# Hybrid decoder trunk: v, gate values and dt computed with tokens on partitions, small matmuls in clusters, output projection in half inputs for six tiles

## The chip, the cores and the metric

One core of one Trainium2 chip runs the whole program in one launch. TensorE (PE) multiplies, VectorE (DVE), ScalarE (ACT) and GpSimd (POOL) work on the results, SyncE (SP) issues the weight transfers. The metric is the device time in microseconds (us) of one execution; the time before is the median of three runs.

## The reference

The trunk has two layers over 512 tokens of width 1024, all in float32: a half-step gated FFN, a mixer, another half-step FFN. The change is in the mixer:

```python
h = rmsnorm(x, mix_norm[l])
proj = h @ w_in[l]        # z 512 | xBC 1024 | dt 8 | q 256 | k 128 | v 128 | u 256 | gv 256
y_ssd = ssd_mixer(z, xBC, dt, ...)       # conv + silu; dt = softplus(dt + bias); chunks of 128 tokens
y_att = rmsnorm(swa_attention(q, k, v, sinks, rel_bias), attn_out_norm[l])
y_sgu = rmsnorm(chunk_sgu(u, gv, ...), sgu_out_norm[l])   # gv = layernorm(gelu(gv)), mixed over tokens
x = x + concat([y_ssd, y_att, y_sgu]) @ w_out[l]
```

In `ssd_mixer`, four chunks of 128 tokens carry a state from one to the next, and the result is multiplied by `silu(z)` and normalised. `swa_attention` works on four blocks of 128 queries.

## The kernel before

**Layout.** The residual lies as eight tiles `xT[j]` of 128 channels by 512 tokens. Each operand of a product is split into a rounded part and a rest (`whi` and `wlo` of the weights, `xhi` and `xlo` of the input: ACT makes the first, L149 and L158, DVE the second, L150 and L159). A product is three matmuls per 128 input channels: whi·xhi (L176), whi·xlo (L177), wlo·xhi (L179). An output tile of the projection, 128 channels by 512 tokens, is thus 24 matmuls of 512 columns.

**Input projection.** `in_products` runs three tiles interleaved over the first six input tiles, then the rest one by one. The order is dt, k, v, q0, q1, eight tiles of xBC, gv0, gv1, u0, u1, z0 to z3. dt is a tile of 16 outputs (rounded part and rest beside each other), 16 matmuls. The RMS factor of the tokens, `R`, comes from squares (ACT), their sum (POOL, L200), a matmul with ones (L217), a power on POOL (L221) and four matmuls that spread it over partitions (L230).

**Turning.** Products come with channels on partitions. dt (L699), v (L858) and the gate values gv (L935) are wanted with tokens on partitions: PE transposes them 128 tokens at a time against the identity, and ACT or DVE read them back.

**Small matmuls.** A list `jobs` hangs work behind each tile's emission. An attention block is scores (L875), softmax on DVE and ACT, transposes (L898), values (L904). A chunk of the SSD is transposes of x (L765) and B (L779), C·B (L776), decay on DVE, POOL and ACT (L784 to L794), the carried state (L801), the new state (L812) and the diagonal part (L807). L957 mixes gate values. L875 uses 64 of the array's rows; L686, L807, L904 and L957 fill 64 of its columns.

**Order.** The Tile framework puts the instructions of each engine in order by its own estimate of when each is ready; each engine then runs its list in that order. So a small matmul stands between product matmuls wherever it was expected to be ready.

**Output projection.** Four output tiles first take input tiles 4 to 7 (attention and gating, 12 matmuls each), while the SSD's norm is finished; then the same four take input tiles 0 to 3, then four tiles take all eight. The SSD's sum of squares (`sst`) is added on POOL.

Of the kernel before, what the change touches and what calls it, by code (L numbers as in the profile page):

```python
# [19 lines left out]
F32 = mybir.dt.float32  # L20
# [6 lines left out]
P = 128  # L27
# [21 lines left out]
XBC_AT, GV_AT, U_AT, Z_AT = 4, 12, 14, 16  # L49
# [3 lines left out]
def trunk(ctx: ExitStack, tc: tile.TileContext, a: dict, out: bass.AP, phases=None):  # L53
# [133 lines left out]

    class Stat:
# [63 lines left out]
    def in_products(tiles, xs, emit, hooks, levels=None, feed=None, ready=2, lead=3, then=None):  # L252
# [29 lines left out]
        for n in range(len(tiles) - lead):  # L282
            wt, m = nxt
            b = accbank()
            product(b[0:m, :], wt, xs, [(k, k) for ks in levels for k in ks], k0, k1)
            if lead + n + 1 < len(tiles):
                nxt = tiles[lead + n + 1]()
            elif then:
                nxt = then()
            emit(lead + n, b)  # L290
# [361 lines left out]
    def mixer(l):  # L652
# [3 lines left out]
        with tc.tile_pool(name="mp", bufs=1) as mp:  # L656
# [37 lines left out]
            def emit_dt(b):  # L694
                dtc = mp.tile([16, T], F32, name="dtc", tag="tmp", bufs=2)
                nc.vector.tensor_tensor(out=dtc, in0=b[0:16, :], in1=R[0:16, :], op=ALU.mult)
                tb = bank()[:, 0:64].rearrange("p (c e h) -> p c e h", c=NB, e=2)
                for c in range(NB):
                    nc.tensor.transpose(tb[:, c, :, :], dtc[:, c * P:(c + 1) * P], ident[0:16, 0:16])  # L699
                v, s, s2, po = (small(n, 32) for n in ("sp_v", "sp_s", "sp_q", "sp_p"))  # L700
                nc.scalar.activation(out=nega, in_=nega, func=AF.Exp)
                nc.vector.tensor_tensor(out=c8(v), in0=tb[:, :, 1, :],
                                        in1=dtb.unsqueeze(1).broadcast_to([P, NB, 8]), op=ALU.add)
                nc.vector.tensor_tensor(out=c8(v), in0=tb[:, :, 0, :], in1=c8(v), op=ALU.add)
# [8 lines left out]
                for n in (15, 13, 11, 9, 7, 5, 3):  # L713
# [6 lines left out]
                                               op0=ALU.mult, op1=ALU.mult)  # L720
                ab = bank()
# [36 lines left out]
            def ssd_chunk(c):  # L758
                if c == 0:
                    nc.scalar.activation(out=eb, in_=eb, func=AF.Exp)  # L760
                cs = slice(c * P, (c + 1) * P)
                h8 = slice(c * 8, c * 8 + 8)
                xb = bank()
                for j in range(4):
                    nc.tensor.transpose(xb[:, j * P:(j + 1) * P], xj[j][:, cs], ident)  # L765
                v64 = lambda t: t.rearrange("p (h d) -> p h d", h=8)
                xdt = t512("xdt", 2)
                nc.vector.tensor_tensor(out=v64(xdt), in0=v64(xb),
                                        in1=dt[:, h8].unsqueeze(2).broadcast_to([P, 8, 64]), op=ALU.mult)
                if c < NB - 1:  # L770
                    xde = t512("xde")
                    nc.vector.tensor_tensor(out=v64(xde), in0=v64(xb),
                                            in1=dtde[:, h8].unsqueeze(2).broadcast_to([P, 8, 64]), op=ALU.mult)
                gb = bank()
                for g in range(2):
                    nc.tensor.matmul(gb[:, g * P:(g + 1) * P], BT[g][:, cs], CT[g][:, cs], start=True, stop=True)  # L776
                if c < NB - 1:
                    for g in range(2):
                        nc.tensor.transpose(gb[:, 256 + g * P:256 + (g + 1) * P], BT[g][:, cs], ident)  # L779
                n = 512 if c < NB - 1 else 256  # L780
                cbt = t512("cbt", 2)
                nc.scalar.copy(out=cbt[:, 0:n], in_=gb[:, 0:n])
                acb = mp.tile([P, 8, P], F32, name="acb", tag="acb", bufs=2)
                nc.gpsimd.dma_start(out=acb, in_=arow[l][h8, :].partition_broadcast(P))  # L784
                dec = []
                for g in range(2):
# [6 lines left out]
                    nc.scalar.activation(out=dg, in_=dg, func=AF.Exp)  # L793
                    nc.vector.tensor_tensor(out=dg, in0=dg,  # L794
                                            in1=cbt[:, g * P:(g + 1) * P].unsqueeze(1).broadcast_to([P, 4, P]),
                                            op=ALU.mult)
                    dec.append(dg)
# [7 lines left out]
                yb = bank()  # L805
                for h in range(8):
                    nc.tensor.matmul(yb[(h % 2) * 64:(h % 2 + 1) * 64, (h // 2) * P:(h // 2 + 1) * P],  # L807
                                     xdt[:, h * 64:(h + 1) * 64], dec[h // 4][:, h % 4, :], start=True, stop=True)
                if c < NB - 1:
# [11 lines left out]
                    state["prev"] = pv  # L821
                for j in range(4):
                    nc.vector.scalar_tensor_tensor(out=xj[j][:, cs], in0=xj[j][:, cs], scalar=vcol(R_DS + l * 4 + j),
                                                   in1=yb[:, j * P:(j + 1) * P], op0=ALU.mult, op1=ALU.add)
# [4 lines left out]

            def emit_z(j, b):  # L830
                z = mp.tile([P, T + 3], F32, name="z", tag=("xc", "cv")[j // 2], bufs=2)[:, 0:T]
                nc.vector.tensor_tensor(out=z, in0=b, in1=R, op=ALU.mult)
                nc.scalar.activation(out=z, in_=z, func=AF.Silu)
                nc.vector.tensor_tensor(out=xj[j], in0=xj[j], in1=z, op=ALU.mult)
                sst.add(xj[j])
# [17 lines left out]
            def emit_v(b):  # L853
                v = t512("v", 2, "tmp")
                nc.vector.tensor_tensor(out=v, in0=b, in1=R, op=ALU.mult)
                tb = bank()
                for c in range(NB):
                    nc.tensor.transpose(tb[:, c * P:(c + 1) * P], v[:, c * P:(c + 1) * P], ident)  # L858
                nc.scalar.copy(out=vt.rearrange("p c d -> p (c d)"), in_=tb)

# [3 lines left out]
            def att_block(n):  # L864
# [26 lines left out]
                nc.vector.reciprocal(out=dn, in_=dn)  # L891
                for kv in range(2):
                    pb = bank()[:, 0:2 * W].rearrange("p (g k q) -> p g k q", g=2, k=nk)
                    for g in range(2):
                        nc.vector.tensor_scalar(out=s[kv][:, g, :], in0=s[kv][:, g, :],
                                                scalar1=dn[:, 2 * kv + g:2 * kv + g + 1], scalar2=None, op0=ALU.mult)
# [3 lines left out]
                    nc.scalar.copy(out=pT, in_=pb)  # L900
                    ob = bank()
# [18 lines left out]
            gvs = []  # L920

            def emit_gv(i, b):
                g = t512("gvt", 2, "tmp")
                nc.vector.tensor_tensor(out=g, in0=b, in1=R, op=ALU.mult)
                nc.scalar.activation(out=g, in_=g, func=AF.Gelu_apprx_tanh)
                gvs.append(g)

            def sgu_norm():
                bks = [bank(), bank()]
                mv = mp.tile([P, NB, 2], F32, name="mv")  # L930
                rs = small("rs", NB)
                for c in range(NB):
                    tb = bks[c // 2][:, (c % 2) * 256:(c % 2 + 1) * 256]
                    for i in range(2):
                        nc.tensor.transpose(tb[:, i * P:(i + 1) * P], gvs[i][:, c * P:(c + 1) * P], ident)  # L935
                    bst = mp.tile([P, 6], F32, name="bst", tag="bst", bufs=2)
                    nc.vector.bn_stats(out=bst, in_=tb)
# [3 lines left out]
                for c in range(NB):  # L941
                    tb = bks[c // 2][:, (c % 2) * 256:(c % 2 + 1) * 256]
                    nc.vector.tensor_scalar(out=gn[:, c, :], in0=tb, scalar1=mv[:, c, 0:1], scalar2=rs[:, c:c + 1],
                                            op0=ALU.subtract, op1=ALU.mult)
# [7 lines left out]
            def sgu_mix(i):  # L952
                b = bank().rearrange("p (c t) -> p c t", c=NB)
# [17 lines left out]
            def mk_dt():  # L971
                raw = load(a["w_dt"][l]).rearrange("p (k n) -> p k n", n=8)
                w = wtile("whi")[:, :KD * 16].rearrange(
                    "p (k n) -> p k n", k=KD)
                nc.scalar.copy(out=w[:, :, 0:8], in_=raw)
                nc.vector.tensor_tensor(out=w[:, :, 8:16], in0=raw, in1=w[:, :, 0:8].bitcast(F32), op=ALU.subtract)
                return (w, None), 16

            jobs = [(mk_dt, emit_dt, [])]
            jobs.append((mk_cols(0), emit_k, []))  # L980
            jobs.append((mk_cols(1), emit_v, []))
            jobs.append((mk_cols(2), lambda b: emit_q(0, b), []))
            jobs.append((mk_cols(3), lambda b: emit_q(1, b), [L(att_block, 0)]))
            after = {0: [L(att_block, 1)], 2: [L(att_block, 2)], 4: [L(att_block, 3)], 5: [sgu_weights],
                     6: [att_stat], 7: [L(ssd_chunk, 0)]}
            for t in range(8):
                jobs.append((mk_cols(XBC_AT + t), lambda b, t=t: emit_xbc(t, b),
                             after.get(t, [])))
            jobs.append((mk_cols(GV_AT), lambda b: emit_gv(0, b), [L(ssd_chunk, 1), ast.start]))
            jobs.append((mk_cols(GV_AT + 1), lambda b: emit_gv(1, b), [L(ssd_chunk, 2), sgu_norm, att_finish]))  # L990
            uj = [(mk_cols(U_AT), lambda b: emit_u(0, b), [L(sgu_mix, 0), L(ssd_chunk, 3)]),
                  (mk_cols(U_AT + 1), lambda b: emit_u(1, b), [L(sgu_mix, 1)])]
            zj = []
# [5 lines left out]
            def emit(n, b):  # L999
                jobs[n][1](b)  # L1000
                for f in jobs[n][2]:
                    f()
# [140 lines left out]
```

## Time and profile before

| | |
|---|---|
| median of three runs (lowest, highest) | 1812.48 us (1812.39, 1815.73) |
| the profiled execution, its span | 1812.49 us, 1810.8 us |
| PE busy, DVE, ACT, POOL | 99%, 74%, 49%, 6% of the span |
| granted TensorE clock, mean | 0.999 |
| mixer of layer 0, of layer 1 (first mixer product to first product of the next FFN) | 358.54 to 559.44, 1248.22 to 1449.74 |

Times of instructions are from the start of the span. A matmul's record runs from its start to a modelled end that lies inside its successor's; how long the engine needs for one in a row of them is the distance between two starts. A matmul of float32 operands leaves two records, one for each of its two passes; a transpose and a product matmul leave one. Some records are missing.

### The profile page before, as it was taken

The numbers are of one execution on the slowest core, as the hardware profiler recorded it, in microseconds if no ns is written. First come the engines' busy times: TensorE is split into PE (matmuls) and PEld (weight loads), VectorE is DVE, ScalarE is ACT, GpSimd is POOL, SyncE is SP. The second block draws the span as 40 slices with busy tenths as digits, with TensorE's granted clock in tenths as the row PEclk, the third lists the DMA queues.
The fourth block names the chain that finished last, engine by engine and source line by source line (L and its number), as shares of the span: only waits on it lengthen the run. The fifth ranks groups of instructions, "written<-read, shape, count | busy, mean of one in ns | idle before, by whom it ended". The sixth has DMA issues, their size and how long they took to land.

```text
span 1810.8 us, 28970 instructions
## 1 busy us (share of the span) xinstructions
PE 1796.4 (99%) x11618; PEld 1614.9 (89%) x11618; DVE 1342.0 (74%) x2075; ACT 884.3 (49%) x1380; POOL 110.7 (6%) x113
## 2 busy tenths in 40 slices
PE   9999999999999999999999999999999999999998
PEld 7899989877888999989989999898788889999886
DVE  7978796568857988886688878855788589887422
ACT  5455563447444545463435555534564445546312
POOL 0000001020221000001000000010102200000000
PEclk9999999999999999999999999999999999999999
DMA  5333333342222233333313333333422223333331
GB/s 176 125 104 106 97 108 111 116 124 72 80 92 77 100 105 105 98 106 114 105 58 117 107 104 108 110 97 106 123 93 70 87 65 117 105 106 105 97 103 47
DMA packets 54963, 183.27 MB, mean 101 GB/s; under 512 B 7211, under 2 KB 9196, under 8 KB 54828
## 3 DMA queue, kind: packets, MB, share of 16 engines
q1 hardware_dynamic: 49484, 172.37, 29.1%
q0 software_dynamic: 1920, 6.59, 1.2%
q10 hardware_dynamic: 3424, 2.46, 0.5%
q8 instruction: 91, 1.49, 0.3%
q14 instruction: 44, 0.36, 0.1%
HBM read 178.48 MB, written 2.92 MB: 100 GB/s over the span
## 4 chain that ended last, share of the span: by engine, by line
PE 88%; DVE 6%; issue 2%; DMA 2%; ACT 1%; POOL 1%; POOLq 0%; ACTq 0%; SPq 0%
PE accb L176 9%; PE accb L177 9%; PE accb L179 9%; PE accb L450 8%; PE accb L452 8%; PE accb L451 8%; PE mxb L452 7%; PE mxb L450 7%; PE mxb L451 7%; PE mxb L1044 1%; PE mxb L176 1%; PE mxb L1043 1%; PE mxb L177 1%; PE mxb L179 1%; PE mxb L1042 1%
## 5 line engine op out<-in xcount | busy, mean ns | idle before, releaser
L450 PE MATMUL accb<-as,whi 128*128 128x256 f32 x1208 | 342.0, 283 | 0.0
L451 PE MATMUL accb<-as,whi 128*128 128x256 f32 x1208 | 341.7, 283 | 0.0
L452 PE MATMUL accb<-as,wlo 128*128 128x256 f32 x1208 | 341.3, 283 | 0.0
L149 ACT CAST whi<-raw 128x1024 fp32r<-128x1024 f32 (+2 forms) x161 | 161.7, 1011 | 293.8 <-PE accb L177 150.8
L150 DVE TENSOR_TENSOR wlo<-raw,whi 128x1024 fp32r<-128x1024 f32 (+2 forms) x161 | 189.0, 1180 | 125.4 <-ACT whi L149 124.6
L176 PE MATMUL accb<-xhi,whi 128*128 128x512 f32 (+1 forms) x712 | 280.8, 395 | 0.0
L177 PE MATMUL accb<-xlo,whi 128*128 128x512 f32 (+1 forms) x712 | 279.6, 393 | 0.0
L179 PE MATMUL accb<-xhi,wlo 128*128 128x512 f32 x696 | 273.0, 393 | 0.4 <-DVE wlo L150 0.3
L450 PEld LDWEIGHTS accb<-as,whi 128*128 128x128 f32 x1208 | 231.9, 192 | 0.9 <-issue 0.5
L451 PEld LDWEIGHTS accb<-as,whi 128*128 128x128 f32 x1208 | 231.9, 192 | 0.3
L452 PEld LDWEIGHTS accb<-as,wlo 128*128 128x128 f32 x1208 | 231.7, 192 | 0.0
L430 DVE TENSOR_TENSOR wlo<-tmp,whi 128x1024 fp32r<-128x1024 f32 x166 | 201.8, 1218 | 37.9 <-ACT whi L424 37.9
L452 PE MATMUL mxb<-as,wlo 128*128 128x256 f32 x784 | 222.1, 283 | 0.9 <-DVE wlo L430 0.9
L450 PE MATMUL mxb<-as,whi 128*128 128x256 f32 x784 | 222.5, 284 | 0.0
L451 PE MATMUL mxb<-as,whi 128*128 128x256 f32 x784 | 221.7, 283 | 0.0
L424 ACT CAST whi<-tmp 128x1024 fp32r<-128x1024 f32 x166 | 173.8, 1051 | 73.3 <-PE accb L177 17.1
L430 DVE TENSOR_TENSOR wlo<-raw,whi 128x1024 fp32r<-128x1024 f32 x83 | 101.6, 1224 | 109.7 <-ACT whi L424 109.7
L177 PEld LDWEIGHTS accb<-xlo,whi 128*128 128x128 f32 (+1 forms) x712 | 132.4, 186 | 29.0 <-issue 1.3
L176 PEld LDWEIGHTS accb<-xhi,whi 128*128 128x128 f32 (+1 forms) x712 | 132.3, 186 | 28.9 <-issue 1.0
L179 PEld LDWEIGHTS accb<-xhi,wlo 128*128 128x128 f32 x696 | 130.7, 188 | 28.9 <-DVE wlo L150 1.5
L452 PEld LDWEIGHTS mxb<-as,wlo 128*128 128x128 f32 x784 | 150.3, 192 | 1.5 <-DVE wlo L430 1.5
L450 PEld LDWEIGHTS mxb<-as,whi 128*128 128x128 f32 x784 | 150.3, 192 | 1.0
(284 smaller groups left out, 3434.0 us busy)
## 6 DMA issues: line engine op xcount, KB each, us to landing
raw<-in_ffn_w_up_dram SPq DMA_DIRECT2D x88, 512.0 KB, 3.5
raw<-in_ffn_w_gate_dram SPq DMA_DIRECT2D x87, 512.0 KB, 3.5
raw<-in_ffn_w_down_dram SPq DMA_DIRECT2D x48, 512.0 KB, 3.7
raw<-in_w_in_dram SPq DMA_DIRECT2D x40, 512.0 KB, 3.5
raw<-in_last_w_down_dram SPq DMA_DIRECT2D x22, 512.0 KB, 3.6
raw<-in_ffn_w_down_dram SPq DMA_DIRECT2D x24, 384.0 KB, 3.0
raw<-in_w_out_dram SPq DMA_DIRECT2D x16, 512.0 KB, 3.5
acb<-arow POOLq DMA_DIRECT2D x8, 512.0 KB, 6.2
```

Of the source, the lines that this page charges most:

```text
L149: pinned(nc.scalar.copy(out=hi[:, c], in_=raw[:, c]))
L150: pinned(nc.vector.tensor_tensor(out=lo[:, c], in0=raw[:, c], in1=hi[:, c].bitcast(F32), op=ALU.subtract))
L176: nc.tensor.matmul(ps, whi[:, i, :], xh, start=(k == first), stop=False)
L177: mm = nc.tensor.matmul(ps, whi[:, i, :], xl, start=False, stop=(wlo is None and k == last))
L179: mm = nc.tensor.matmul(ps, wlo[:, i, :], xh, start=False, stop=(k == last))
L424: nc.scalar.copy(out=hi, in_=self.srcs[i])
L430: nc.vector.tensor_tensor(out=lo, in0=self.srcs[i], in1=self.his[i].bitcast(F32), op=ALU.subtract)
L450: nc.tensor.matmul(ps, whi[:, c, :], xh, start=(start and c == 0), stop=False, skip_group_check=True)
L451: nc.tensor.matmul(ps, whi[:, c, :], xl, start=False, stop=False, skip_group_check=True)
L452: mm = nc.tensor.matmul(ps, wlo[:, c, :], xh, start=False, stop=(c == 3), skip_group_check=True)
L1042: nc.tensor.matmul(o, hh[:, ts], wh[:, 0, ds], start=False, stop=False)
L1043: nc.tensor.matmul(o, hl[:, ts], wh[:, 0, ds], start=False, stop=False)
```

## The change

- dt, v and gv no longer are tiles of the list. `token_products` computes them first: the stationary operand is 128 tokens of xhi or xlo, the moving one 392 weight columns (v 128, gv 256, dt 8), for four groups of tokens: 4 × 8 × 3 = 96 matmuls of 392 columns, in four accumulator banks at once. The factor of the token is then a scalar per partition, and 12 DVE instructions put the results where they are used. The transposes L699, L858 and L935 and the copies behind them are gone. The weights come as four transfers of 128 × 784.
- The remaining 17 tiles run one by one. Attention blocks and SSD chunks are cut in pieces (`att_scores`, `att_turn`, `att_values`; `ssd_decay`, `ssd_begin`, `ssd_end`), and on PE a job's pieces are queued behind the tile's last product.
- z is applied to all four tiles after the last one (`gate`), with the sum of squares on DVE.
- Six output tiles take input tiles 4 to 7 first, with weights loaded in halves of 128 × 512.

```diff
+            def token_products(between, then):
+                bs = [accbank()[:, 0:N_TOK] for c in range(NB)]
+                nxt = mk_tok(0)
+                for i in range(KD // 2):
+                    hi, lo = nxt
+                    if i in between:
+                        between[i]()
+                    nxt = mk_tok(i + 1) if i + 1 < KD // 2 else then()
+                    for c in range(NB):
+                        for j in range(2):
+                            k = 2 * i + j
+                            xh, xl = (t[:, c * P:(c + 1) * P] for t in xs[k])
+                            nc.tensor.matmul(bs[c], xh, hi[:, j, :], start=(k == 0), stop=False)
+                            nc.tensor.matmul(bs[c], xl, hi[:, j, :], start=False, stop=False)
+                            mm = nc.tensor.matmul(bs[c], xh, lo[:, j, :], start=False, stop=(k == KD - 1))
+                    latest[0] = mm.ins
...
+            jobs = [(mk_cols(0), emit_k, [sgu_norm]),
+                    (mk_cols(1), lambda b: emit_q(0, b), []),
+                    (mk_cols(2), lambda b: emit_q(1, b), [dt_sums])]
+            for t, more in enumerate(([L(att_scores, 0)], [], [L(att_turn, 0), L(att_scores, 1)], [L(att_values, 0)],
+                                      [L(att_turn, 1), L(att_scores, 2)],
+                                      [L(att_values, 1), sgu_weights, L(late, ssd_decay, 0)],
+                                      [L(att_turn, 2), L(att_scores, 3), L(late, ssd_decay, 1)], [L(att_values, 2)])):
+                jobs.append((mk_cols(XBC_AT + t), lambda b, t=t: emit_xbc(t, b), more))
+            jobs += [(mk_cols(U_AT), lambda b: emit_u(0, b), [L(att_turn, 3), L(ssd_begin, 0)]),
+                     (mk_cols(U_AT + 1), lambda b: emit_u(1, b),
+                      [L(att_values, 3), L(ssd_end, 0), L(ssd_begin, 1), L(ssd_decay, 2), L(sgu_mix, 0)])]
+            for j, more in enumerate(([L(ssd_end, 1), L(ssd_begin, 2), L(ssd_decay, 3), att_stat, L(sgu_mix, 1)],
+                                      [L(ssd_end, 2), L(ssd_begin, 3), ast.start, gst.start],
+                                      [L(ssd_end, 3), att_finish, L(finish, gst, u, R_GN + l * 2, 6)],
+                                      [L(gate, i) for i in range(4)])):
+                jobs.append((mk_cols(Z_AT + j), lambda b, j=j: emit_z(j, b), more))
             def emit(n, b):
                 jobs[n][1](b)
-                for f in jobs[n][2]:
-                    f()
+                with behind():
+                    for f in jobs[n][2]:
+                        f()
...
+            def gate(j):
+                nc.vector.tensor_tensor(out=xj[j], in0=xj[j], in1=zs[j], op=ALU.mult)
+                sst.add(xj[j], nc.vector)
...
+            LEAD = 6
+            early, late_k, every = range(4, 8), range(0, 4), range(KD)
+            steps = [(j, early) for j in range(LEAD)] + [(j, late_k) for j in range(LEAD)]
+            steps += [(j, every) for j in range(LEAD, KD)]
```

How the instructions now stand, at three places of layer 0. On PE where the mixer begins, with dt's tile and its transposes (`dtc`) in the kernel before:

```order
L176 MATMUL accb<-xhi,whi 16x512
L177 MATMUL accb<-xlo,whi 16x512
...
L230 MATMUL mxb<-ident,rcol 128x128 x4
L176 MATMUL accb<-xhi,whi 128x512
...
L699 MATMUL mxb<-ident,dtc 128x16 x4
```

and in the changed kernel:

```order
L1013 MATMUL accb<-whi,xhi 128x392
L1014 MATMUL accb<-whi,xlo 128x392
L1015 MATMUL accb<-wlo,xhi 128x392
...
L227 MATMUL mxb<-ones,sqs 128x1 x4
...
L240 MATMUL mxb<-ident,rcol 128x128 x4
L177 MATMUL accb<-xhi,whi 128x512
```

The 96 matmuls of 392 columns stand first, 72 of them ahead of the sum of squares (L227) and 24 between it and the spreading (L240); the transposes of dt are gone.

On PE in the attention blocks, before (`s` are the softmax's results, `pT` their transposes):

```order
L898 MATMUL mxb<-ident,s 128x128 x4
L177 MATMUL accb<-xlo,whi 128x512
...
L904 MATMUL mxb<-pT,vt 64x128 x4
L898 MATMUL mxb<-ident,s 128x128 x4
L176 MATMUL accb<-xhi,whi 128x512
...
L904 MATMUL mxb<-pT,vt 64x128 x4
L875 MATMUL mxb<-kT,q 128x256 x4
L176 MATMUL accb<-xhi,whi 128x512
```

and now:

```order
L924 MATMUL mxb<-ident,s 128x128 x8
L895 MATMUL mxb<-kT,q 128x256 x4
L180 MATMUL accb<-xhi,wlo 128x512
...
L936 MATMUL mxb<-pT,vt 64x128 x8
L700 MATMUL mxb<-wT,lnb 64x128 x4
L177 MATMUL accb<-xhi,whi 128x512
```

Both halves of a block's transposes, and both of its values, stand together: one group each where there were two.

On ACT where the last tile of xBC (`C`, made by a silu) meets the first chunks, before (`gvt` are gate values, `cbt` is the copy of C·B):

```order
L754 ACTIVATE C_3869<-cv 128x512
L749 ACTIVATE cv<-xc,col 128x512
L149 CAST whi<-raw 128x1024
L754 ACTIVATE C_3870<-cv 128x512
L925 ACT_TABLE_LOAD
L925 ACTIVATE gvt<-gvt 128x512
L782 COPY cbt<-mxb 128x512
```

and now:

```order
L757 ACTIVATE cv<-xc,col 128x512
L969 ACT_TABLE_LOAD
L969 ACTIVATE u_3878<-u_3878 128x512
L926 COPY pT<-mxb 128x512
L779 ACT_TABLE_LOAD
L779 ACTIVATE acb<-acb 128x512 x2
...
L762 ACT_TABLE_LOAD
L762 ACTIVATE C_3870<-cv 128x512
L969 ACT_TABLE_LOAD
L969 ACTIVATE u_3879<-u_3879 128x512
L796 COPY cbt<-mxb 128x512
```

Between the convolution's first step (`cv`) and the silu of the second C tile there now stand a gelu, two exponentials of the decay and three loads of a function table, where no load stood before; a layer has 21 such loads, where it had 12.

## Rows read from the trace of the kernel before

**Rows 1.** The page's part 1: busy us, share of the span, instructions.
```profile
PE 1796.4 (99%) x11618; PEld 1614.9 (89%) x11618; DVE 1342.0 (74%) x2075; ACT 884.3 (49%) x1380; POOL 110.7 (6%) x113
```
**Rows 2.** Busy time by stretch: both mixers, then chunks of layer 0.
```profile
core 0: us, PE busy (x) PEld busy (x) DVE busy (x) ACT busy (x) POOL busy (x), PEclk, DMA share, GB/s
358.54:559.44 200.90, 199.26 (x1069) 158.37 (x1068) 146.53 (x268) 102.43 (x160) 38.84 (x37) 1.00 0.30 95
1248.22:1449.74 201.52, 199.29 (x1069) 158.33 (x1068) 146.66 (x268) 102.45 (x160) 37.48 (x37) 1.00 0.30 94
445.45:493.00 47.55, 47.33 (x323) 38.28 (x323) 41.39 (x75) 19.76 (x27) 9.87 (x9) 1.00 0.24 79
```
**Rows 3.** PE in order of time, products: start, us, engine, line, operation, tiles, shape.
```profile
376.28 0.39 PE L176 MATMUL accb<-xhi,whi 128*128 128x512 f32 x1
376.51 0.39 PE L177 MATMUL accb<-xlo,whi 128*128 128x512 f32 x1
376.74 0.39 PE L179 MATMUL accb<-xhi,wlo 128*128 128x512 f32 x1
```
**Rows 4.** PE in order of time, the FFN's products of 256 columns.
```profile
620.16 0.28 PE L450 MATMUL mxb<-as,whi 128*128 128x256 f32 x1
620.28 0.28 PE L451 MATMUL mxb<-as,whi 128*128 128x256 f32 x1
620.40 0.28 PE L452 MATMUL mxb<-as,wlo 128*128 128x256 f32 x1
```
**Rows 5.** PE in order of time, spreading of the factor and products of dt's tile.
```profile
370.46 1.05 PE L230 MATMUL mxb<-ident,rcol 128*128 128x128 f32 x8
371.27 0.48 PE L176 MATMUL accb<-xhi,whi 128*16 128x512 f32 x1
371.59 0.40 PE L177 MATMUL accb<-xlo,whi 128*16 128x512 f32 x1
371.82 0.40 PE L176 MATMUL accb<-xhi,whi 128*16 128x512 f32 x1
```
**Rows 6.** PE in order of time around the transposes of dt.
```profile
373.44 0.39 PE L179 MATMUL accb<-xhi,wlo 128*128 128x512 f32 x1
373.76 0.41 PE L699 MATMUL mxb<-ident,dtc 16*128 16x16 f32 x4
374.11 0.50 PE L176 MATMUL accb<-xhi,whi 128*128 128x512 f32 x1
374.44 0.39 PE L177 MATMUL accb<-xlo,whi 128*128 128x512 f32 x1
```
**Rows 7.** PE in order of time around two transposes of gate values.
```profile
478.36 0.39 PE L176 MATMUL accb<-xhi,whi 128*128 128x512 f32 x1
478.59 0.38 PE L935 MATMUL mxb<-ident,gvt 128*128 128x128 f32 x2
478.73 0.48 PE L177 MATMUL accb<-xlo,whi 128*128 128x512 f32 x1
479.05 0.39 PE L179 MATMUL accb<-xhi,wlo 128*128 128x512 f32 x1
```
**Rows 8.** PE in order of time, half an attention block.
```profile
413.21 0.40 PE L179 MATMUL accb<-xhi,wlo 128*128 128x512 f32 x1
413.54 0.66 PE L904 MATMUL mxb<-pT,vt 128*64 128x128 f32 x8
414.13 0.66 PE L898 MATMUL mxb<-ident,s 128*128 128x128 f32 x4
414.54 0.48 PE L176 MATMUL accb<-xhi,whi 128*128 128x512 f32 x1
414.86 0.39 PE L177 MATMUL accb<-xlo,whi 128*128 128x512 f32 x1
```
**Rows 9.** PE's waits in layer 1's mixer: us in total, times, longest us.
```profile
PE mxb L898 <- DVE s L895: 0.9, 1, 0.9
PE mxb L904 <- ACT pT L900: 0.7, 1, 0.7
PE mxb L217 <- POOL sqs L200: 0.4, 1, 0.4
```
**Rows 10.** ACT in order of time, a load of a function table.
```profile
403.28 1.28 ACT L754 ACT_TABLE_LOAD   x1
404.58 0.63 ACT L754 ACTIVATE xs<-cv 128x512 f32<-128x512 f32 x1
```

## Prediction on record

> **What bounds the kernel now.** First the page's busy shares: PE is busy for 99% of the span [rows 1], which says little, since a matmul's record reaches over its successor's start. So I read starts instead. In a run of products the starts stand 0.23 us apart (376.28, 376.51, 376.74) although each record is 0.39 us long [rows 3]; the exact pitch, from long runs of them, is 0.227. The question is then how much of a mixer is such a run. A mixer has 20 tiles of 24 matmuls and 8 output tiles of 24: 672 × 0.227 = 152.5 us, and 16 narrow matmuls of dt's tile at 0.23, 3.7 us. That is 156 of the 201 us that it takes [rows 2]; the other 45 are small matmuls, what it costs to change between them and products, and waits. VectorE is busy for 147 of the 201 us and ScalarE for 102, so neither bounds the mixer as a whole; in the stretch of the SSD's chunks, VectorE comes to 41.4 of 47.6 us [rows 2], and there it can. The waits are few: PE's list for the mixer of layer 1 has three over half a microsecond or near it, 0.9 and 0.7 us in attention and 0.4 us for the SSD's sum of squares on POOL [rows 9]; layer 0 has the first and the last alike. So the mixer is bound by what PE is given to do, and an edit there is worth the PE time that it removes, as long as the others keep up. The clock is granted fully (1.00 in both mixers [rows 2], the 2.4 GHz level) and PE has no long idle stretch in which it could fall.
>
> **The change part by part**, for one layer, in PE time.
>
> *Token products.* Removed are three tiles, 72 × 0.227 = 16.3 us, and dt's 16 × 0.233 = 3.7 us [rows 5]: 20.1 us. Added are 96 matmuls of 392 columns, which the trace does not have. Its neighbours are 512 columns at 0.227 [rows 3] and 256 columns at 0.12 [rows 4], both with a weight load of 128 columns for each matmul; these bound it, at 96 × 0.12 = 11.5 and 96 × 0.227 = 21.8 us, so at a gain of 8.5 or a loss of 1.7. I take the line through the two, 0.12 + 136 × (0.227 − 0.12)/256 = 0.177 us, so 17.0 us: a gain of 3.1 us. The line is not free: its constant part is 0.013 us per matmul.
> The Trainium skill (TensorE: Matmul & The Clock Gate, section Back-to-back issue gap) gives columns over 2.4 GHz plus 2.5 ns, which makes 166 ns of 392 columns. Here 256 columns take 0.12 us where that rule says 0.109, and 512 take 0.227 where it says 0.216 [rows 3, 4], so the rows decide; by the rule the gain would be 1.1 us larger in a layer.
>
> *Transposes.* dt's four: from 373.44 to 374.44 there are two products' pitches and this group, 1.00 − 0.45 = 0.55 us [rows 6]. Gate values: 478.36 to 479.05 is 0.69 − 0.45 = 0.24 us for two [rows 7], eight are 0.95. v: four at that price, 0.48. Together 2.0 us gone. The reading back goes from DVE and ACT too, and 12 small DVE instructions and a new chain of evictions come in at the end of the token products. These four banks are needed by the tiles k, q0, q1 and the first of xBC, one each 5.4 us, so the eviction has the length of a product to hide in; if that cover were short, the tile k would wait for its bank.
>
> *Clusters.* Merging groups of transposes saves nothing in itself: two of them between products cost 0.12 us each, about what one costs in a row. What costs is a change of the array's shape. In half an attention block, 413.21 to 414.86, 1.65 us hold two pitches (0.45), four transposes (0.48) and four values matmuls on 64 columns [rows 8]. These run in pairs side by side; four full ones take 0.81 us (370.46 to 371.27 [rows 5]), so four in pairs 0.4. The 0.32 us left are two changes of shape, 0.16 each. Along PE's order I count 43 changes in a mixer before and 28 now; two of the 43 are in dt's 0.55 us. 13 × 0.16 = 2.1 us gone. The bounds are 0 and 0.2 us per change.
>
> *Waits.* The sum of squares on VectorE: the wait of 0.4 us for POOL [rows 9] goes; the sum now has 36 products, 8.2 us, between the end of z3 and its matmul, where 24 stood before. The two attention waits should go as well, 1.0 us in one layer and 1.6 in the other: between scores and transposes there are now 47 to 56 products where 22 to 48 stood. I book nothing for them, because the chunks will bring waits of about that size: C's last tile comes late on ScalarE, behind three loads of tables, and begins the first chunk about when PE gets there; then the first chunk's decay products on VectorE come about half a microsecond late. My estimate of these from the durations in line is 1 to 1.5 us.
>
> *Six tiles by halves.* No matmul more or less. 12 weight loads of half size in place of six add a fixed part to six ScalarE and six VectorE instructions, hidden under products of 2.7 us each. What is worth something is the cover: 72 products instead of 48 while the SSD's norm is finished, 16.3 us for 10.9. Before, PE waited there for nothing but the sum, so the cover as such is worth nothing more.
>
> Sum for a layer: 3.1 + 2.0 + 2.1 + 0.4 = 7.6 us, for two layers 15.2. The profiled execution took 1812.5 us, as the median: 1797.3 us; I say 1797. From the start of the mixer on, tiles are prefetched two ahead as before, so the FFNs around it should not change.
>
> **The rivals.**
> 1. *VectorE sets the pace in the chunks.* For it: 41.4 us of work in 47.6 us [rows 2], and now the stretch on PE becomes shorter by some 3 us (its gate transposes and part of the changes of shape) while VectorE's work stays, with turns of shorter slack between the end of one chunk and the next. Against it: by durations in line, each chunk's decay products are ready within the product of a tile. If VectorE held the stretch at its old length, 3 us a layer are lost: 1803.
> 2. *A matmul of 392 columns costs as one of 512*, if weight load or bank change set the pitch. Against it: 256 columns run at 0.12 us with the same load [rows 4]. Price 96 × 0.05 = 4.8 us a layer: 1807.
> 3. *Slower: ScalarE's table loads.* A layer has nine more, at 1.28 us [rows 10] 11.5 us, 23 in all. They stand in the chunks, where exponentials, gelus and silus of three stages are interleaved; where a chunk's C, its decay or a gate waits behind one, PE stands still, since each engine keeps its order. If all were on the path the time would be 1797 + 23 = 1820; from two thirds of them on the kernel is slower than before. Against it: ScalarE was busy for 19.8 of 47.6 us in that stretch [rows 2], so most loads fall into its idle time.
> The Trainium skill (ScalarE: Activation LUTs, section What ACT_TABLE_LOAD costs) names 2.66 us for a switch, with a drain. Here the instruction after a load starts 1.30 us after the load's start [rows 10], so I go by that; by the page this rival would cost twice as much.
> 4. *All old waits go and no new one comes.* Then 1.0 + 1.6 us more are gained, and if the changes of shape cost 0.2 us another 1: about 1793; with a pitch nearer to that of 256 columns, 1790.
>
> **How the numbers follow.** The forecast has 0.58, rival 1 0.20, rival 2 0.05, rival 3 0.07, rival 4 0.10. The forecast's own spread is 1794 to 1801. The range reaches to 1789 below, which takes in rival 4, and to 1807 above, with rivals 1 and 2 and the lighter part of 3. A difference of 0.2%, 3.6 us, can be told from no change: faster means under 1808.9, slower over 1816.1. Faster: the forecast, rival 4, and most of 1 and 2, 0.58 + 0.10 + 0.16 + 0.03 = 0.87. Slower: most of rival 3, 0.06. No change: the rest, 0.07.
>
> **What would show it.** In the profile of the changed kernel: the token products' starts 0.177 us apart; no group of transposes before the attention blocks; the mixers 193 to 194 us long; PE's list of waits without POOL's sum, with at most some 2 us a layer, its largest entries for C, for the decay products or for a copy behind them. I am wrong if PE waits for VectorE or ScalarE for more than 3 us in a layer, if the tile k waits for its bank, or if the start of the next FFN moves relative to the mixer's end.

## The result and the profile after

The changed kernel takes 1794.32 us, median of 4 runs (1794.26 to 1795.78), against 1813.03 us of the kernel before: a ratio of 0.9896, 95% interval 0.9879 to 0.9913, 18.7 us less where the sum of terms had 15.2. Its profiled execution took 1794.26 us, with a span of 1792.2.

The page's part 1 of the changed kernel, which answers to [rows 1]:

```profile
PE 1780.5 (99%) x11602; PEld 1618.1 (90%) x11602; DVE 1336.9 (75%) x2105; ACT 907.8 (51%) x1412; POOL 97.3 (5%) x107
```

Busy time with the columns of [rows 2]: both mixers, then the stretch of time that held the chunks in the kernel before, then the stretch from the first of the chunks' matmuls on PE to the last one now:

```profile
358.41:550.27 191.86, 191.44 (x1061) 159.89 (x1060) 143.76 (x283) 113.95 (x176) 31.57 (x34) 1.00 0.33 100
1239.09:1430.94 191.85, 191.43 (x1062) 159.88 (x1060) 144.12 (x283) 113.93 (x176) 31.43 (x34) 1.00 0.32 100
445.45:493.00 47.55, 47.55 (x326) 39.28 (x325) 41.23 (x80) 34.99 (x52) 10.29 (x11) 1.00 0.14 45
457.65:497.38 39.73, 39.73 (x293) 33.32 (x292) 33.73 (x62) 24.97 (x34) 12.01 (x12) 1.00 0.17 54
```

Both mixers are now 191.9 us long, 9.0 and 9.7 us less than [rows 2]; that is the whole gain. The third row is the same time by the clock as in [rows 2], but no longer the same work: the chunks begin later and are packed closer. From their first matmul on PE to their last they took this long in the kernel before:

```profile
446.81:492.48 45.67, 45.45 (x304) 36.82 (x303) 39.65 (x73) 18.45 (x25) 9.87 (x9) 1.00 0.25 82
```

So 45.7 us have become 39.7. VectorE is busy for 33.7 of them (39.7 of 45.7 before), ScalarE for 25.0 (18.5 before): VectorE has about the same share of a shorter stretch, ScalarE more work in less time.

PE in order of time at the start of the token products, which answers to [rows 3]:

```profile
358.41 0.34 PE L1013 MATMUL accb<-whi,xhi 128*128 128x392 f32 x1
358.58 0.34 PE L1014 MATMUL accb<-whi,xlo 128*128 128x392 f32 x1
358.76 0.34 PE L1015 MATMUL accb<-wlo,xhi 128*128 128x392 f32 x1
358.94 0.34 PE L1013 MATMUL accb<-whi,xhi 128*128 128x392 f32 x1
```

Starts are 0.17 to 0.18 us apart; over all 192 of both layers the mean is 0.178. The list of PE's waits in the mixer of layer 1, which answers to [rows 9], has one row, and that of layer 0 the same one:

```profile
PE mxb L924 <- DVE s L913: 0.4, 1, 0.4
```

The two attention waits and POOL's are gone, and in their place stands one: the transposes (L924) of attention's block 2 wait for its scaled softmax. Starts on PE give each wait its whole price (a step between two starts, less the pitch of 0.227). All steps over 0.345 us summed come to 2.45 and 3.20 us in the two mixers before, and to 0.59 and 0.58 us now.

### The profile page after: what moved, and what is told of

It reads as the page before. It is cut to its first block, busy times and chain, and to the rows that moved or that the text cites. A ratio compares the mean times of both kernels' runs of the same rounds, so it can differ in the third digit from the quotient of the medians.

```text
span 1792.2 us, 29027 instructions
## 1 busy us (share of the span) xinstructions
PE 1780.5 (99%) x11602; PEld 1618.1 (90%) x11602; DVE 1336.9 (75%) x2105; ACT 907.8 (51%) x1412; POOL 97.3 (5%) x107
## 4 chain that ended last, share of the span: by engine, by line
PE 91%; DVE 6%; ACT 2%; issue 1%; DMA 0%; POOL 0%; POOLq 0%; SPq 0%; ACTq 0%
PE accb L177 9%; PE accb L180 9%; PE accb L178 9%; PE accb L464 8%; PE accb L466 8%; PE accb L465 8%; PE mxb L466 7%; PE mxb L464 7%; PE mxb L465 7%; PE mxb L177 1%; PE mxb L178 1%; PE mxb L180 1%; PE mxb L1112 1%; PE mxb L1111 1%; PE mxb L1110 1%; PE accb L1112 1%
## 5 line engine op out<-in xcount | busy, mean ns | idle before, releaser
L150 ACT CAST whi<-raw 128x1024 fp32r<-128x1024 f32 (+2 forms) x167 | 157.8, 952 | 273.3 <-PE accb L178 112.2
L151 DVE TENSOR_TENSOR wlo<-raw,whi 128x1024 fp32r<-128x1024 f32 (+2 forms) x167 | 183.3, 1105 | 128.0 <-ACT whi L150 127.9
L177 PE MATMUL accb<-xhi,whi 128*128 128x512 f32 x616 | 242.7, 395 | 0.0
L180 PE MATMUL accb<-xhi,wlo 128*128 128x512 f32 x616 | 240.8, 391 | 0.4 <-DVE wlo L151 0.3
L178 PE MATMUL accb<-xlo,whi 128*128 128x512 f32 x616 | 240.7, 391 | 0.0
L464 PEld LDWEIGHTS mxb<-as,whi 128*128 128x128 f32 x784 | 150.3, 192 | 1.0
L465 PEld LDWEIGHTS mxb<-as,whi 128*128 128x128 f32 x784 | 150.4, 192 | 0.5
L177 PEld LDWEIGHTS accb<-xhi,whi 128*128 128x128 f32 x616 | 115.7, 188 | 26.1 <-issue 3.1
L180 PEld LDWEIGHTS accb<-xhi,wlo 128*128 128x128 f32 x616 | 115.7, 188 | 26.2 <-DVE wlo L151 1.5
```

Source lines behind the costliest of these rows:

```text
L150: pinned(nc.scalar.copy(out=hi[:, c], in_=raw[:, c]))
L151: pinned(nc.vector.tensor_tensor(out=lo[:, c], in0=raw[:, c], in1=hi[:, c].bitcast(F32), op=ALU.subtract))
L177: nc.tensor.matmul(ps, whi[:, i, :], xh, start=(k == first), stop=False)
L178: mm = nc.tensor.matmul(ps, whi[:, i, :], xl, start=False, stop=(wlo is None and k == last))
L180: mm = nc.tensor.matmul(ps, wlo[:, i, :], xh, start=False, stop=(k == last))
L464: nc.tensor.matmul(ps, whi[:, c, :], xh, start=(start and c == 0), stop=False, skip_group_check=True)
```

## Experiments

Mixers are compared below from their first product to the end of the last residual add, which is 1.4 us more than the stretches above: before 202.27 and 202.88 us, after 193.23 and 193.22.

**The token products alone.** The kernel before with the new token products, and its other small matmuls where they were:

```diff
+            jobs = [(mk_cols(0), emit_k, [sgu_norm]),
+                    (mk_cols(1), lambda b: emit_q(0, b), [dt_sums]),
+                    (mk_cols(2), lambda b: emit_q(1, b), [L(att_block, 0)])]
...
-            in_products([j[0] for j in jobs], xs, emit, {(0, 2): st.start, (1, 0): make_R})
+            makers = [j[0] for j in jobs]
+            nxt = token_products({3: st.start}, makers[0])
+            make_R()
+            one_by_one(makers, 0, nxt, xs, list(range(KD)), emit)
```

> The kernel before with the token products alone: v, gate values and dt come from 392-column products, the gate values' transposes, v's and dt's are gone; the small matmuls stay where the kernel before has them (whole attention blocks and whole chunks behind one tile), the output projection and the POOL sum are the old ones. Theory (the gain is PE time removed in three separate parts, plus waits): token products 3.1 us and transposes 2.0 us a layer go, with two changes of shape 0.3; about 5.4 us a layer, 10.8 us in all, so 1802 us against 1813; attention's waits of 1.0 to 1.6 us a layer and POOL's of 0.5 us are still there. Rival (the layout is all, clusters give nothing): 1795 us. Rival (the clusters and their waits are nearly all): 1809 us or more.

> The token products alone again, now with chunk 3 ahead of the first gate as the reference wants it (in the run before, the first gate came ahead of chunk 3), and with the granted clock looked at beside each time, since that run was spread over 10 us with clocks from 0.995 to 0.999. Theory (token products, transposes and two changes of shape, 5.4 us a layer, less the new waits that the run before showed: some 1.2 us more for POOL's sum and 0.6 us for a split input late in the output projection, a layer): mixers of 197 to 198 us against 201, and at a clock of 0.999 about 1805 us. Rival (the layout is all of the gain): mixers of 192 us, 1795 us.

The first run took 1810.94 us (1805.54 to 1815.77, clocks 0.999 down to 0.995), ratio 0.9988, interval 0.9977 to 0.9999; its mixers are 199.24 and 199.44 us long in the profile, 4.1 and 4.4 of them waits. In its kernel the first gate stands ahead of chunk 3, so that it computes something else than the reference, with the same matmuls; the second run has them in order. The second took 1807.8 us (1805.99 to 1808.75), ratio 0.9964, interval 0.9951 to 0.9978; mixers 201.74 and 198.89. Without the waits the first run's mixers are 195.1 and 195.0 us, and the second mixer of the second run is 195.2, against 199.8 and 199.7 before: the layout alone takes 4.5 to 4.7 us off PE's work, where 5.4 was expected. But PE now comes to attention sooner and waits longer there, and in the second run it pays twice. PE in order of time in that run:

```profile
401.54 0.39 PE L180 MATMUL accb<-xhi,wlo 128*128 128x512 f32 x1
404.54 0.97 PE L894 MATMUL mxb<-ident,s 128*128 128x128 f32 x2 [2.61 <-DVE s L891]
405.16 0.78 PE L177 MATMUL accb<-xhi,whi 128*128 128x512 f32 x1
405.74 0.63 PE L178 MATMUL accb<-xlo,whi 128*128 128x512 f32 x1
406.16 0.63 PE L180 MATMUL accb<-xhi,wlo 128*128 128x512 f32 x1
406.59 0.63 PE L177 MATMUL accb<-xhi,whi 128*128 128x512 f32 x1
```

PE stands for 2.61 us, and behind that the products start 0.43 us apart instead of 0.227: the lower clock level, 1.2 GHz, granted 0.83 on the mean from 400 to 410 us. So the layout alone gave two thirds of what PE's own work lost, but only about a third of the gain in time, or less: 2.2 and 6.5 us of 18.7 by the two ratios, 3.0 and 3.4 of 9.0 and 9.7 by the first run's mixers. The rest came with the other edits, 2.4 us a layer of PE's work and 3.5 to 3.9 of waits. Of these waits, 1.7 us stood in the output projection (POOL's sum 1.2, a split input 0.6), so the clusters alone are not credited with all of them; no run here has the clusters alone.

**The output projection by four tiles again**, in the changed kernel:

```diff
-            LEAD = 6
...
+            in_products([mk_o(j) for j in range(KD)], yo, emit_o,
+                        {(0, 2): sst.start, (0, 3): lambda: finish(sst, xj, R_SN + l * 4, 0)},
+                        [[4, 5, 6, 7], [0, 1, 2, 3]], ready=1, lead=4)
```

> The changed kernel with the old output projection: four tiles by halves and 48 products of cover instead of six and 72. Theory (the halves are worth nothing as such): the matmul of the sum of squares now has 24 products in front of it, 5.5 us from the end of z3, and by the trace of the changed kernel the sum on VectorE is ready 6.1 us after it: a wait of 0.4 to 0.6 us a layer, 1795.2 us. Rival (the norm's four split inputs, 6.2 us on VectorE after the spread, come late for the second halves, which need the last of them 4.8 us after the spread): 1.4 us more a layer, 1798 us.

1796.2 us (1794.86 to 1796.61); each mixer 0.75 us longer (194.00, 193.94). PE's waits in layer 0, and PE in order of time at the sum's matmul (L227) and the spreading (L240):

```profile
PE mxb L240 <- POOL rcol L231: 0.6, 1, 0.6
PE mxb L924 <- DVE s L913: 0.4, 1, 0.4
```

```profile
511.83 0.94 PE L227 MATMUL mxb<-ones,sqs 128*128 128x1 f32 x8
514.19 1.16 PE L240 MATMUL mxb<-ident,rcol 128*128 128x128 f32 x8 [0.59 <-POOL rcol L231]
```

The wait has the size expected but another place: not the sum of squares, but the power that POOL computes from it (1.01 us). In this run only three products stand between the sum's matmul and the spreading, where the kernel before had twelve and the changed kernel has 24. So taking the halves out costs 0.75 us a layer, which the prediction's "the cover as such is worth nothing more" did not foresee; whether the old projection would wait as well with twelve products there is not shown.

**The sum of squares on POOL again**, in the changed kernel, and on VectorE in the kernel before:

```diff
-                sst.add(xj[j], nc.vector)
+                sst.add(xj[j])
```

> The changed kernel with the squares added on POOL again. Theory (the longer cover alone hides POOL's additions): in the changed kernel the last square is ready at about 509.2 us, three additions of 1.29 us in a row end at about 511.0, the matmul that wants them starts at 512.9: no wait, 1794.3 us, so VectorE's sum is worth nothing once there are 36 products in front. Rival (the sum on VectorE is what removed POOL's wait): 0.5 us a layer come back, 1795.3 us or more.

> The kernel before with the one edit that the squares of the SSD's gated output are added on VectorE instead of POOL. Theory (the prediction's term): the wait of PE for POOL's sum, a step of 0.77 and 0.76 us where 0.23 is the pitch, goes: 0.5 us a layer, 1.1 us in all, 1812 us. Rival (the addition comes in VectorE's queue behind a split of weights and is no earlier): nothing, 1813 us.

The first: 1793.94 us (1793.70 to 1795.38), mixers 193.21 and 193.23, and no wait for the sum; POOL's last addition ends at 512.41 us and PE's matmul starts at 512.52, so the longer cover is just long enough. The second: 1812.49 us, ratio 0.9994, interval 0.9986 to 1.0003. POOL's wait is gone there too; PE at the sum's matmul, before and in this run:

```profile
519.33 1.05 PE L217 MATMUL mxb<-ones,sqs 128*128 128x1 f32 x8 [0.38 <-POOL sqs L200]
519.66 0.95 PE L217 MATMUL mxb<-ones,sqs 128*128 128x1 f32 x8
```

The mixers are 201.69 and 202.63 us long, 0.57 and 0.25 less than before (in the second, attention's waits are 0.2 us longer). So the sum on VectorE is worth about what the prediction gave it in the kernel before, by one profile; the medians can't tell that much from nothing. With the longer cover it is worth nothing more: either edit takes the same wait away.

**Token products of 512 columns**, the weights padded with zeros:

```diff
-N_TOK = 392
+N_TOK = 512
```

> The changed kernel with the token weights padded by 120 columns of zeros, so that the 96 token products a layer have 512 columns. Theory (a product's pitch goes by its columns): from 0.178 to 0.227 us, 4.7 us a layer, 9.4 us in all, 1803.7 us. Rival (weight load, banks or the splits set the pace of the token products): less than 3 us in all, 1794 to 1797 us.

1804.83 us (1803.59 to 1805.17), mixers 198.08 and 198.01 us, 4.8 a layer longer, as expected from 96 times 0.049. A product's pitch goes by its columns.

**The price of a change of shape.** Small matmuls of constants in the middle of the tiles:

```diff
             b = accbank()
-            product(b[0:m, :], wt, xs, [(k, k) for k in ks], ks[0], ks[-1])
+            product(b[0:m, :], wt, xs, [(k, k) for k in ks[:h]], ks[0], ks[-1])
+            e = accbank()
...
+                            o, w = e[g * 64:(g + 1) * 64, i * P:(i + 1) * P], ones[:, 0:64]
+                        else:
+                            o, w = e[:, (2 * i + g) * P:(2 * i + g + 1) * P], ones
+                        mm = nc.tensor.matmul(o, w, ident, start=True, stop=True)
+            product(b[0:m, :], wt, xs, [(k, k) for k in ks[h:]], ks[0], ks[-1])
```

> The changed kernel with four small matmuls of constants in the middle of each of the 17 tiles of a mixer that follow the token products: in layer 0 on 64 columns in two pairs side by side, in layer 1 on the full array. They add work and change no output. Theory (a change of the array's shape costs 0.16 us, full matmuls in between cost their own time alone): layer 0 gets 17 x (4 x 0.06 + 2 x 0.16) = 9.5 us, layer 1 gets 17 x 4 x 0.11 = 7.5 us; the mixers are 201.4 and 199.4 us long. Rival (a change of shape costs nothing and the rest of the half attention block was something else): 4.1 us in layer 0, 7.5 in layer 1. Rival (leaving a run of products costs the same whatever the small matmul's shape): both get 0.3 us a tile on top, 9.5 and 12.6 us.

> The probe again, with the counts set right: a float32 matmul on the full array is two passes of 0.1 us, so four of them took 0.90 us with what it costs to leave and rejoin the products, and four in pairs on 64 columns 0.81 us. Now twelve instead of four in the middle of each of the 17 tiles of a mixer (and in no other tile), narrow in layer 0, full in layer 1; twelve against four gives the price of one and what is left at zero. Theory (a change of shape costs 0.16 us, a pair on 64 columns runs side by side): one narrow matmul 0.10 us, left over 0.4 us (two changes and 0.09 that the full ones cost as well), so 1.6 us a tile, 27.5 us a mixer; full 0.20 us each, left over 0.09, so 2.5 us a tile, 42.7 us a mixer; mixers of 220.7 and 235.9 us. Rival (pairs don't run side by side but narrow matmuls are simply 0.2 us): 2.4 us a tile, 41 us in layer 0 as well, and no price for a change of shape.

The second probe took 1869.84 us, its mixers 222.16 and 238.73 where 220.7 and 235.9 were expected. The first expectation had the matmuls' own time wrong by half (a float32 matmul is two rows in the trace, and I took one row for it), and the probe also stood in some FFN tiles, so the total of 1843.11 us is not to be used; its single insertions are. PE in order of time around twelve narrow matmuls (24 rows) and twelve full ones in the second probe:

```profile
388.19 0.39 PE L180 MATMUL accb<-xhi,wlo 128*128 128x512 f32 x1
388.51 1.53 PE L311 MATMUL accb<-ident,ones 128*64 128x128 f32 x24
389.97 0.50 PE L177 MATMUL accb<-xhi,whi 128*128 128x512 f32 x1
390.31 0.40 PE L178 MATMUL accb<-xlo,whi 128*128 128x512 f32 x1
390.55 0.40 PE L180 MATMUL accb<-xhi,wlo 128*128 128x512 f32 x1
390.78 0.40 PE L177 MATMUL accb<-xhi,whi 128*128 128x512 f32 x1
...
1290.63 0.39 PE L180 MATMUL accb<-xhi,wlo 128*128 128x512 f32 x1
1290.86 2.84 PE L311 MATMUL accb<-ident,ones 128*128 128x128 f32 x24
1293.45 0.48 PE L177 MATMUL accb<-xhi,whi 128*128 128x512 f32 x1
1293.77 0.39 PE L178 MATMUL accb<-xlo,whi 128*128 128x512 f32 x1
```

From 388.19 to 390.78 are four pitches (0.91) and 1.68 us for the narrow ones; from 1290.63 to 1293.77 two pitches (0.45) and 2.69 us for the full ones. The first probe gives 0.81 and 0.90 us for four. All 17 insertions of a layer agree within 0.01 us. The line through four and twelve: a narrow matmul 0.11 us and 0.37 us left over; a full one 0.22 us and 0.01 us left over. So going to 64 columns and back costs 0.18 us each way, a full matmul among products costs its own time alone, and the prediction's 0.16 stood a little low. The Trainium skill (TensorEngine Tiling (Array Packing), section Key Properties) says that a change of tiling mode drains TensorE, without a price; the probe fits that and gives one.

**More table loads on ScalarE**, two more functions ahead of each chunk's copy:

```diff
+                nc.scalar.activation(out=swap[:, 0:1], in_=swap[:, 0:1], func=AF.Silu)
+                nc.scalar.activation(out=swap[:, 0:1], in_=swap[:, 0:1], func=AF.Exp)
```

> The changed kernel with a silu and an exponential of one column of zeros on ScalarE ahead of the copy that each chunk's decay products wait for, so two more table loads in each of the four chunks of a layer, up to eight more in a layer at 1.28 us, 10 us. No output changes. Theory (ScalarE's loads fall into its idle time, 114 of 192 us are busy): at most 1.5 us a layer comes back as waits of PE, 1794 to 1797 us. Rival (the loads stand on the path that PE waits for): 8 to 10 us a layer, 1811 to 1815 us.

1793.88 us (1793.80 to 1795.59). A mixer has 28 loads now, where the changed kernel has 21 and the kernel before 12; eight of them are the new ones, in groups of lines on ScalarE (count, busy us, mean ns):

```profile
L797 ACT ACT_TABLE_LOAD x4 | 5.1, 1283 | 0.1
L798 ACT ACT_TABLE_LOAD x4 | 5.1, 1283 | 0.1
```

Nine more microseconds of loads a layer on ScalarE, and the mixers stay at 193.27 and 193.28 us. The Trainium skill (ScalarE: Activation LUTs, section What ACT_TABLE_LOAD costs) has 1283 ns for the load, as measured here, and 1380 more for a drain; here no time on PE came of either.

**Two entries of the table of jobs moved**, to take away the wait that is left, together and each alone:

```diff
-            for t, more in enumerate(([L(att_scores, 0)], [], [L(att_turn, 0), L(att_scores, 1)], [L(att_values, 0)],
+            for t, more in enumerate(([L(att_scores, 0)], [L(late, ssd_decay, 0)], [L(att_turn, 0), L(att_scores, 1)], [L(att_values, 0)],
...
-                                      [L(att_values, 1), sgu_weights, L(late, ssd_decay, 0)],
+                                      [L(att_values, 1), sgu_weights],
...
-            for j, more in enumerate(([L(ssd_end, 1), L(ssd_begin, 2), L(ssd_decay, 3), att_stat, L(sgu_mix, 1)],
+            for j, more in enumerate(([L(ssd_end, 1), L(sgu_mix, 1), L(ssd_begin, 2), L(ssd_decay, 3), att_stat],
```

> The changed kernel with two entries of its table of jobs moved: the decay of chunk 0 four tiles earlier, behind attention's first block, and the second spatial mix right behind the 64-column matmuls of chunk 1. Theory (what is left of waits is the turn of block 2, 0.59 us a layer, late since chunk 0's decay, 0.68 and 1.12 us on VectorE, and a split stand in front of its softmax; and two more changes of shape at 0.16 us go): 0.9 us a layer, 1.8 us in all, 1792.5 us, with no wait of PE over 0.2 us in a mixer. Rival (the wait moves to the turn of block 0 or 1, whose softmax is ready just in time as well): 0.3 us a layer, 1793.7 us.

> One of the two moves of the run before alone: the decay of chunk 0 four tiles earlier. In the program's order the 64-column mix stays behind chunk 2's first half, and the eight small matmuls of the two sums of squares now stand in a row behind chunk 3's first half, so that 36 small matmuls follow each other without a product; in the changed kernel two products stand among them. Theory 1 (the run before lost what it gained to the clock, which fell to 0.53 for 3.5 us right behind such a stretch): the wait of 0.59 us a layer for attention's turn goes, but the clock falls behind the long stretch in some runs and costs about 1.5 us each time: clocks of 0.996 to 0.998 and 1794 to 1798 us, 1793.1 us where it doesn't fall. Theory 2 (the fall was chance, or came from the mix): clocks of 0.999 and 1793.1 us in nearly all runs.

> The other move alone: the second spatial mix right behind the 64-column matmuls of chunk 1. In the program's order three products now stand ahead of the two sums of squares and four between them, more than in the changed kernel. Theory 1 (the clock falls behind long stretches of small matmuls): clocks of 0.999 in nearly all runs; two changes of shape a layer fewer at 0.18 us and attention's wait of 0.59 us as before: 1793.6 us. Theory 2 (the mix next to the 64-column matmuls is what makes the clock fall): clocks of 0.997 and 1796 us.

Both moves: 1796.31 us (1793.30 at a clock of 0.999; the other four at 0.996 and 0.997, 1796.16 to 1798.35). No wait is left, and layer 1's mixer is 192.62 us long, but layer 0's is 194.28, since the clock fell there (column PEclk, before DMA share and GB/s):

```profile
488.00:492.30 4.30, 4.27 (x30) 3.69 (x30) 4.30 (x11) 2.96 (x5) 0.00 (x0) 0.99 0.01 4
492.30:495.80 3.50, 3.50 (x10) 2.70 (x9) 0.78 (x4) 0.00 (x0) 2.48 (x2) 0.53 0.26 75
```

Seven steps there are 0.43 us long, 1.5 us lost. In the 7.5 us before, PE did small matmuls and only six products, and no wait is listed. The decay alone: 1793.63 us (1793.36 to 1794.74), no wait, mixers 192.59 and 192.65 us, 0.6 a layer shorter than the changed kernel's, and clocks of 0.998 and 0.999, though the longest row of small matmuls without a product is 5.6 us in it, and the row ahead of the fall in the run before was 5.1 us. So the theory that such a row makes the clock fall did not hold; what made it fall in the run before is open. The mix alone: 1796.61 us (1795.58 to 1798.82), mixers 194.07 and 194.08. Theory 2 named the time, but not the cause: the profiled clock is 0.999, and PE waits. Its list in layer 0:

```profile
PE mxb L793 <- DVE yf L825: 0.5, 1, 0.5
PE mxb L924 <- DVE s L913: 0.4, 1, 0.4
PE mxb L227 <- DVE prev L837: 0.2, 1, 0.2
```

Two VectorE instructions of the mix (0.74 and 0.68 us) now stand ahead of chunk 2's, and the chunk behind it comes late. That is the prediction's first rival, VectorE as the pace of the chunks, one move away.

## Why the prediction was right, and what it had wrong

- **Token products**, 3.1 us forecast. Right: 0.178 us a product where the line through 256 and 512 columns gave 0.177, so 96 of them take 17.1 us for 20.1. The 512-column run rules out rival 2. The Trainium skill (TensorE: Matmul & The Clock Gate, section Back-to-back issue gap) makes 0.166 us of it, by its formula for an isolated matmul; the rows decide.
- **Transposes and changes of shape**, 2.0 and 2.1 us forecast. Right together: of the 9.0 and 9.7 us, waits are 1.9 and 2.6, so PE's own work shrank by 7.2 and 7.0, and token products, transposes and changes had been forecast at 7.2. One change costs 0.18 us by the probe, so thirteen come to 2.4, about what separates the token products alone from the whole change; the layout's part fell 0.7 us or more short of its 5.4, so the sum came out partly by luck. Which of its terms fell short is not shown, nor is 0.18 us the price at every place: with 30 and 26 changes a layer in place of 28 (decay alone, mix alone) PE's work without the waits stayed at 192.6 us.
- **Waits**, 0.4 us forecast. This is the term that was mis-sized: 1.9 and 2.6 us went. The step that failed is "I book nothing for them, because the chunks will bring waits of about that size": the waits for C and for the decay products, 1 to 1.5 us, did not come. The table loads behind which C was to be late fit into ScalarE's idle time, as the run with seven more showed, and the only new wait is in attention (0.6 us), late behind chunk 0's decay on VectorE; it went when the decay was moved. The actual time is nearer to rival 4's 1793 us than to the 1797 forecast, and rival 4's condition came true but for this one new wait.
- **The sum of squares.** Its wait went, and VectorE's sum alone takes it away in the kernel before, as forecast. What the prediction did not see is that the longer cover of the six halves does the same by itself, so the two do not add up.
- **Rival 1** did not happen (the chunks' stretch became 5.9 us shorter), but there is little room: 1.4 us of VectorE's work put ahead in the chunks brought about 0.9 us of waits a layer. **Rival 3** fell: 9 us of loads a layer more cost nothing.
- **What would show it.** The tile k did not wait for its bank, no group of transposes stands ahead of attention, and the next FFN starts as before. The mixers, 191.9 us, are 1 to 2 us shorter than the 193 to 194 named.

## What to carry over

A change that shortens PE's work brings PE sooner to data that other engines still prepare: price the layout and the order of the work separately, since here the layout alone gave two thirds of the PE work saved and about a third of the time. Before booking new waits against old ones, look whether the engine that should be late has idle time in that stretch; before adding up what edits are worth, ask whether two of them take away the same wait, as the sum on VectorE and the longer cover did. Small matmuls on half the array are cheap in a row (0.11 us against 0.22) and dear alone (0.37 us for going there and back), so they belong together.

## What the runs showed of the hardware

- A full-array float32 matmul between float32r products costs only its own time (0.01 us left over); going to 64 columns and back in the middle of a tile costs 0.37 us.
- One wait of 2.6 us was followed by the 1.2 GHz level for some 3 us, so it cost about half as much again; and the clock also fell to that level once, for 3.5 us, behind 7.5 us of small matmuls and six products in which PE's busy records leave almost no gap.
- Several kernels of nearly the same work were spread over 3 to 10 us with granted clocks of 0.995 to 0.999. Differences under 2 us are told here by the length of the mixers in one profile of each kernel and by its waits, not by the medians.
